# Two token mixers' TensorE work: a hand-written list of steps becomes threads woven into one fixed order, with 16-wide block inverses

## The chip, the cores and the metric

One NeuronCore of one Trainium2 chip runs the whole program in one launch. The metric is the device time of one execution in microseconds (us). Times of a kernel are shown as the median of several executions; one more execution is profiled, and the rows below are from that one.

## The reference

The input is one sequence of 512 frames with 1024 features, all float32. There are two layers. Each layer is a half-weighted SwiGLU feed-forward block (1024 to 2 x 2816 to 1024), a block with two token mixers side by side, and a second feed-forward block. The mixer block, shortened:

```
z = rmsnorm(h) @ w_in[l]                      # columns: r,k,v,w,a,g | q,k,v,o,i,f | two gates of 1024
y_a = rwkv7(...)                              # 8 heads of 64: S = S*w - (S kk) b + v k ; y = S r, frame by frame
y_b = mlstm(...)                              # 4 heads of 128: causal, with input and forget gates, normalised
u = sigmoid(g_a)*(y_a @ br_a) + sigmoid(g_b)*(y_b @ br_b)
h = h + u @ w_out
```

After RWKV7 and mLSTM each head is standardised and gated. The RWKV7 recurrence is evaluated here in chunks of 64 frames, which needs the inverse of a triangular 64x64 matrix for each head and chunk.

## The kernel before

Activations lie transposed: features on the 128 partitions, the 512 frames along the free dimension. A large product is a *projection*: 128 output features from 1024 inputs, eight k-steps into one PSUM bank. For precision each operand is split into a rounded high part and a remainder, so a k-step is three matmuls of 128x512 (L389 to L391). `weights` loads 512 KB of raw weights (two buffers) on SyncE's queue; `cut` makes the high part on ScalarE (L353) and the remainder on VectorE, or on GpSimd while `self.mixing` is set (L354). The split parts of two projections are held at a time. Projections write into three PSUM banks ("mm"), everything else on TensorE into five ("mx").

Between the feed-forward blocks, `mixers` runs. It has 47 projections a layer: one for mixed small columns, two for low-rank inputs, twelve for RWKV (r, k, v for four pairs of heads p), sixteen for mLSTM (q, k, v, o for four heads) and sixteen merge gates. The steps are:

- P (`rwkv_in`) makes decays, keys and receptances of a head pair, with a long chain on VectorE (L800 to L822). X (`rwkv_chunks`) forms the chunk matrices (L845, evacuated at L848 and L849) and transposes (L605). I (`rwkv_inverse`) sends 32x32 blocks through DRAM so that each partition holds whole blocks, inverts them in 31 rounds of two VectorE operations (L884, L886), and sends them back in two layouts, one by way of `td` into t1p. J (`rwkv_merge`) joins 32x32 blocks into 64x64 ones (L902, L906). O (`rwkv_out`) applies the inverse, forms transitions (L938) and runs the recurrence over the chunks (L946, L948, L949, L953). Y (`rwkv_gated`) standardises and gates.
- M, V, S, H make q and k with a short convolution (L659 to L667), the values (ScalarE copy at L672, then transposes), the output gate, and one whole mLSTM head. R computes the mLSTM gates (slab at L645). G is a merge gate's projection, kept in DRAM.

Buffers of the RWKV steps exist twice (`r_set[p % 2]`). A list of steps for each layer, `ORDERS`, sets the order in which they are emitted, with eleven gates among them in layer 0 and five in layer 1; the rest of the gates follow after the last step. The framework's scheduler then orders each engine's queue itself, by emission order, readiness and its own cost model, TensorE's too. At run time every engine takes its queue in order.

## Time and profile before

| | us |
|---|---|
| median of 3 executions | 2565.57 |
| their range | 2559.49 to 4713.14 |
| the profiled execution | 2561.73 |
| its span, first to last instruction | 2560.0 |
| TensorE busy, matmuls | 2455.2 |
| VectorE busy | 1388.7 |
| ScalarE busy | 1050.1 |
| GpSimd busy | 316.0 |

PE is TensorE's matmuls, DVE is VectorE, ACT is ScalarE, POOL is GpSimd; L12 is line 12 of the kernel. Ends of matmuls are modelled by the profiler and overlap the next start, so their spacing is read from the starts. PEclk is the mean granted share of TensorE's clock. A float32 matmul that is not split shows as two records. One of the three executions stands far off the other two and is no measure of the kernel.

### The profile page before, as it was taken

What the parts mean: (1) busy time and instruction counts of PE and PEld (TensorE: products, weight loads), DVE (VectorE), ACT (ScalarE), POOL (GpSimd) and SP (SyncE); (2) the same over time, 40 slices, a digit from 0 to 9 for tenths busy, and PEclk for the clock granted to TensorE, in tenths of its full rate; (3) what the DMA queues carried; (4) which work ended last, traced back from release to release, by engine and by line L of the source; (5) the groups of instructions that cost most, each with busy time, mean ns of one, the idle gap of its engine ahead of it and who ended that gap; (6) DMA issues with size and microseconds to landing.
All of it is one profiled execution on the core that took longest, in us unless ns stands there. A gap on an engine that the chain in (4) does not pass through costs nothing. (4 is left out here: it accounts for less than half of the span.)

```text
span 2560.0 us, 31793 instructions
## 1 busy us (share of the span) xinstructions
PE 2455.2 (96%) x12114; PEld 1983.7 (77%) x12114; DVE 1388.7 (54%) x2421; ACT 1050.1 (41%) x1783; POOL 316.0 (12%) x291
## 2 busy tenths in 40 slices
PE   8999999898989999999999999988999999999997
PEld 7888887676667888888888888767677788888886
DVE  5444445777776644444444434478887555444433
ACT  5333335444546343333343333453555354433322
POOL 0000014322320010000000000143232001000012
PEclk9999999888899999999999999998999999999999
DMA  4222444313332422233332324332213233223232
GB/s 159 93 97 97 116 120 126 103 34 83 105 100 76 147 99 93 97 99 96 94 99 99 99 90 113 117 105 81 80 49 97 77 128 128 95 99 99 92 96 85
DMA packets 127033, 253.46 MB, mean 99 GB/s; under 512 B 55680, under 2 KB 58368, under 8 KB 126880
## 3 DMA queue, kind: packets, MB, share of 16 engines
q1 hardware_dynamic: 126256, 249.79, 31.1%
q8 instruction: 95, 1.56, 0.3%
q10 hardware_dynamic: 624, 1.64, 0.2%
q14 instruction: 58, 0.48, 0.1%
HBM read 230.94 MB, written 20.45 MB: 98 GB/s over the span
## 5 line engine op out<-in xcount | busy, mean ns | idle before, releaser
L353 ACT CAST whi<-wraw 128x512 fp32r<-128x512 f32 (+1 forms) x800 | 485.2, 610 | 1019.8 <-PE mm L390 957.2
L389 PE MATMUL mm<-xh,whi 128*128 128x512 f32 x2160 | 857.2, 397 | 6.0 <-ACT whi L353 5.8
L390 PE MATMUL mm<-xl,whi 128*128 128x512 f32 x2160 | 855.4, 396 | 0.3 <-DVE xl L426 0.2
L391 PE MATMUL mm<-xh,wlo 128*128 128x512 f32 x2160 | 853.4, 395 | 2.2 <-DVE wlo L354 1.3
L354 DVE TENSOR_TENSOR wlo<-wraw,whi 128x512 fp32r<-128x512 f32 (+1 forms) x656 | 458.5, 699 | 542.7 <-ACT whi L353 536.6
L389 PEld LDWEIGHTS mm<-xh,whi 128*128 128x128 f32 x2160 | 411.1, 190 | 95.6 <-ACT whi L353 8.5
L391 PEld LDWEIGHTS mm<-xh,wlo 128*128 128x128 f32 x2160 | 410.6, 190 | 89.3 <-DVE wlo L354 2.2
L390 PEld LDWEIGHTS mm<-xl,whi 128*128 128x128 f32 x2160 | 411.2, 190 | 87.8 <-issue 1.4
L389 PE MATMUL mm<-hh,whi 128*128 128x512 f32 x704 | 273.9, 389 | 0.0
L390 PE MATMUL mm<-hl,whi 128*128 128x512 f32 x704 | 273.9, 389 | 0.0
L391 PE MATMUL mm<-hh,wlo 128*128 128x512 f32 x704 | 273.9, 389 | 0.0
L354 POOL TENSOR_TENSOR wlo<-wraw,whi 128x512 fp32r<-128x512 f32 x144 | 205.4, 1434 | 360.9 <-ACT whi L353 338.6
L438 POOL TENSOR_TENSOR acc<-acc,sq 128x512 f32<-128x512 f32 x36 | 47.9, 1330 | 971.3 <-ACT sq L436 971.3
L390 PEld LDWEIGHTS mm<-hl,whi 128*128 128x128 f32 x704 | 132.2, 188 | 27.7
L391 PEld LDWEIGHTS mm<-hh,wlo 128*128 128x128 f32 x704 | 132.2, 188 | 27.6
L389 PEld LDWEIGHTS mm<-hh,whi 128*128 128x128 f32 x704 | 132.2, 188 | 27.0
L884 DVE TENSOR_TENSOR pr<-ti,mxs 128x16 f32<-128x16 f32 (+30 forms) x248 | 136.9, 552 | 6.5 <-POOL mxs L881 1.2
L469 DVE TENSOR_TENSOR t<-mm,rstd 128x512 f32<-128x512 f32 x88 | 60.8, 691 | 138.7 <-PE mm L391 127.7
L473 DVE TENSOR_TENSOR t<-mm,t 128x512 f32<-128x512 f32 x88 | 60.8, 691 | 132.3 <-PE mm L391 127.7
L886 DVE TENSOR_REDUCE ti<-pr 128x8 f32<-128x16 f32 (+30 forms) x248 | 72.1, 291 | 5.6
L471 ACT ACTIVATE t<-t 128x512 f32<-128x512 f32 x88 | 55.8, 634 | 29.4 <-DVE t L469 29.2
L418 DVE TENSOR_TENSOR hl<-t,hh 128x512 fp32r<-128x512 f32 x88 | 60.9, 692 | 9.9 <-ACT hh L417 2.3
(244 smaller groups left out, 2252.1 us busy)
## 6 DMA issues: line engine op xcount, KB each, us to landing
wraw<-wi SPq DMA_DIRECT2D x94, 512.0 KB, 3.3
wraw<-f2i SPq DMA_DIRECT2D x88, 512.0 KB, 3.2
wraw<-f1i SPq DMA_DIRECT2D x86, 512.0 KB, 3.3
wraw<-f1o SPq DMA_DIRECT2D x32, 512.0 KB, 3.6
wraw<-f2o SPq DMA_DIRECT2D x32, 512.0 KB, 3.5
wraw<-br SPq DMA_DIRECT2D x16, 512.0 KB, 3.3
wraw<-wo SPq DMA_DIRECT2D x16, 512.0 KB, 3.3
wraw<-f1o SPq DMA_DIRECT2D x16, 384.0 KB, 3.2
```

The costliest lines, as they stand in the source:

```text
L353: nc.scalar.copy(out=hi, in_=raw)
L354: eng.tensor_tensor(out=lo, in0=raw, in1=hi.bitcast(F32), op=ALU.subtract)
L389: nc.tensor.matmul(ps, lhsT=hi, rhs=xh, start=first, stop=False)
L390: nc.tensor.matmul(ps, lhsT=hi, rhs=xl, start=False, stop=False)
L391: nc.tensor.matmul(ps, lhsT=lo, rhs=xh, start=False, stop=last)
L418: nc.vector.tensor_tensor(out=lo, in0=x, in1=hi.bitcast(F32), op=ALU.subtract)
L438: eng.tensor_tensor(out=self.acc, in0=self.acc, in1=sq, op=ALU.add)
L469: nc.vector.tensor_tensor(out=g, in0=pg, in1=self.rstd, op=ALU.mult)
L471: nc.scalar.activation(out=s, in_=g, func=AF.Silu)
L473: nc.vector.tensor_tensor(out=p, in0=pu, in1=s, op=ALU.mult)
L884: nc.vector.tensor_tensor(out=pr[:, :, 0 : i + 1], in0=ti[:, 0 : i + 1, :].rearrange("m j c -> m c j"), in1=mx[:, 0 : i + 1, i].unsqueeze( ...
L886: nc.vector.tensor_reduce(out=ti[:, i, :], in_=pr[:, :, 0 : i + 1], axis=mybir.AxisListType.X, op=ALU.add)
```

## The change

The list of steps goes. Each of the four head pairs, the common part, the mLSTM heads, the mLSTM projections, the mLSTM gates and the merge gates becomes a generator, a thread. The new class `Weave` runs them while the program is built. It keeps a planned time for TensorE (`t`) and one for VectorE's queue (`dve`). A thread emits a step, says how long TensorE needs for it (`pe`) or what latency and VectorE time follow (`mark`), and yields what it waits for: a planned time, a flag, a lock on a buffer, or a projection. The first ready thread by rank goes on; while none is ready, one k-step of the current projection is emitted. The merge gates have the last rank and only fill. TensorE's queue is then bound to the order of emission (`manual_schedule`); the other queues stay with the scheduler.

The blocks that are inverted by rounds become 16x16, with 15 rounds; pairs of them are joined to 32x32 by two more sets of small matmuls, and the transposed blocks that came by way of `td` are now made by VectorE's block transpose. The remainder of the weights is always taken on VectorE. The first matmul of each recurrence step (L946) is issued for all chunks ahead into one bank, `sums`, and the step's two others follow it chunk by chunk. The `sums` helper's operands get fixed tiles under a lock.

```diff
-ORDERS = (
-    "G0 P0 G1 S0 G2 X0 G3 G4 P1 G5 G6 X1 I0 G7 V0 R0 J0 O0 Y0 M0 I1 P2 X2 J1 G8 H0 "
...
+class Weave:
...
+    STEP = 0.69
+    def __init__(self, trunk):
+        self.trunk = trunk
+        self.t = self.dve = 0.0
+        self.threads, self.held, self.flags, self.small = [], set(), {}, False
+    def add(self, rank, gen, filler=False):
+        self.threads.append([rank, gen, ("at", 0.0), filler])
+    def mark(self, latency, busy):
+        start = max(self.t, self.dve)
+        self.dve = start + busy
+        return start + latency
+    def pe(self, us):
+        self.t += us + (0.0 if self.small else 0.1)
+        self.small = True
+    def set(self, flag, when=None):
+        self.flags[flag] = self.t if when is None else when
...
+    def ready(self, want):
+        kind, x = want
+        if kind == "at":
+            return x <= self.t
+        if kind == "lock":
+            return x not in self.held
+        if kind == "flag":
+            return x in self.flags and self.flags[x] <= self.t
+        return False
+    def resume(self, th, value=None):
+        try:
+            th[2] = th[1].send(value)
+        except StopIteration:
+            self.threads.remove(th)
+    def run(self):
+        trunk = self.trunk
+        job = None
+        self.threads.sort(key=lambda th: th[0])
+        while job or any(not th[3] for th in self.threads):
+            th = next((th for th in self.threads if self.ready(th[2])), None)
+            if th is not None:
+                if th[2][0] == "lock":
+                    self.held.add(th[2][1])
+                self.resume(th)
+                continue
+            if job is None:
+                th = next((th for th in self.threads if th[2][0] == "proj"), None)
+                if th is not None:
+                    job = [th, trunk.weights(th[2][1]), trunk.mm(), 0]
+                    th[2] = ("job", None)
+                    self.mark(0.0, 1.4)
+            if job is not None:
+                th, w, ps, k = job
+                trunk.product(ps, w, k, trunk.xh[:, k, :], trunk.xl[:, k, :], k == 0, k == KD - 1)
+                self.t += self.STEP + (0.1 if self.small else 0.0)
+                self.small = False
+                job[3] += 1
+                if job[3] == KD:
+                    job = None
+                    self.resume(th, ps)
+                continue
+            times = [th[2][1] for th in self.threads if th[2][0] == "at"]
+            times += [self.flags[th[2][1]] for th in self.threads if th[2][0] == "flag" and th[2][1] in self.flags]
+            self.t = min(times)
...
-        eng = nc.gpsimd if self.mixing else nc.vector
         nc.scalar.copy(out=hi, in_=raw)
-        eng.tensor_tensor(out=lo, in0=raw, in1=hi.bitcast(F32), op=ALU.subtract)
+        nc.vector.tensor_tensor(out=lo, in0=raw, in1=hi.bitcast(F32), op=ALU.subtract)
...
-        steps = {
-            "P": self.rwkv_in, "X": self.rwkv_chunks, "I": self.rwkv_inverse, "J": self.rwkv_merge, "O": self.rwkv_out, "Y": self.rwkv_gated, "M": self.mlstm_in, "V": self.mlstm_values, "S": self.mlstm_output, "H": self.mlstm_head,
-            "G": self.gate_spilled, "R": lambda _: self.mlstm_gates(),
-        }
-        self.mixing = True
-        order = ORDERS[l].split()
-        for s in order:
-            steps[s[0]](int(s[1:]))
...
+        wv = self.wv = Weave(self)
+        wv.add(-1, self.common())
+        for p in range(4):
+            wv.add(p, self.rwkv(p))
+        wv.add(8, self.mlstm_heads())
+        wv.add(9, self.mlstm_projections())
+        wv.add(10, self.mlstm_gates())
+        wv.add(20, self.gates_spilled(early), True)
+        with self.tc.manual_schedule(engines={mybir.EngineType.PE}):
+            wv.run()
...
+    def gates_spilled(self, early):
+        yield "flag", "rows"
+        for i in range(16):
+            ps = yield "proj", self.src[f"g{'ab'[i % 2]}{i // 2}"]
+            g = self.tmp(f"t{1 + i % 2}", 1)
+            self.gate(ps, g)
+            self.nc.sync.dma_start(out=self.gd[i], in_=g)
+            early.add(i)
...
+        yield "at", wv.mark(16.0, 8.0)
         ps = self.mx()
         self.transposes(ps, [slab[:, P * j : P * j + P] for j in range(4)])
...
+    def mlstm_projections(self):
+        nc, l, src, wv = self.nc, self.l, self.src, self.wv
+        yield "flag", "rows"
+        for h in range(4):
+            if h > 0:
+                yield "flag", f"qk{h - 1}"
+            for j, n in enumerate("qk"):
+                i = 4 * j + h
+                ps = yield "proj", src[f"m{n}{h}"]
...
+                qk = wv.mark(7.0, 4.7)
...
+    def rwkv(self, p):
+        wv = self.wv
+        yield "flag", "wa"
+        yield "lock", f"set{p % 2}"
+        yield "lock", "in"
+        yield from self.rwkv_in(p)
+        yield from self.rwkv_chunks(p)
+        wv.free("in")
+        yield "lock", "inverse"
+        yield from self.rwkv_inverse(p)
+        yield from self.rwkv_merge(p)
+        wv.free("inverse")
+        yield "lock", "out"
+        yield from self.rwkv_out(p)
+        wv.free("out")
+        yield "lock", "gated"
+        yield from self.rwkv_gated(p)
+        wv.free("gated")
+        wv.free(f"set{p % 2}")
...
+        self.ready_mx = wv.mark(7.5, 3.4)
+        at = wv.t + 3.0
         for q in range(2):
+            yield "at", at
             Q = slice(4 * q, 4 * q + 4)
             ps = self.mx()
             self.transposes(ps, [bk[:, c, :, :] for c in range(4 * q, 4 * q + 4)])
...
+        nc, wv = self.nc, self.wv
         avr, mn, rbx, s3, dc = self.r_set[p % 2]
-        mx, ti, tz, pr, t1p = self.r_mx, self.r_ti, self.r_tz, self.r_pr, self.r_t1p
-        for g in range(4):
-            nc.sync.dma_start(out=mx[g::4], in_=self.mxd[p])
-        nc.gpsimd.memset(mx.rearrange("m j i -> m (j i)")[:, 0::33], 1.0)
-        nc.gpsimd.tensor_copy(out=ti, in_=self.tid)
-        for i in range(1, 32):
-            nc.vector.tensor_tensor(out=pr[:, :, 0 : i + 1], in0=ti[:, 0 : i + 1, :].rearrange("m j c -> m c j"),
-                                    in1=mx[:, 0 : i + 1, i].unsqueeze(1).broadcast_to([P, 8, i + 1]), op=ALU.mult)
-            nc.vector.tensor_reduce(out=ti[:, i, :], in_=pr[:, :, 0 : i + 1], axis=mybir.AxisListType.X, op=ALU.add)
-        nc.vector.tensor_copy(out=tz, in_=ti.rearrange("m j c -> m c j"))
-        td, zd = self.td[p], self.zd[p]
-        nc.sync.dma_start(out=td, in_=ti[0:64])
+        mx, mt, tz, pr = self.r_mx, self.r_mt, self.r_tz, self.r_pr
+        for g in range(2):
+            nc.sync.dma_start(out=mx[g::2], in_=self.mxd[p])
+        nc.gpsimd.memset(mx.rearrange("m j i -> m (j i)")[:, 0::17], 1.0)
+        nc.scalar.copy(out=mt, in_=mx.rearrange("m j i -> m i j"))
+        nc.gpsimd.tensor_copy(out=tz, in_=self.tid)
+        for i in range(1, 16):
+            nc.vector.tensor_tensor(out=pr[:, :, 0 : i + 1], in0=tz[:, :, 0 : i + 1],
+                                    in1=mt[:, i, 0 : i + 1].unsqueeze(1).broadcast_to([P, 8, i + 1]), op=ALU.mult)
+            nc.vector.tensor_reduce(out=tz[:, :, i], in_=pr[:, :, 0 : i + 1], axis=mybir.AxisListType.X, op=ALU.add)
+        zd = self.zd[p]
         nc.sync.dma_start(out=zd, in_=tz)
-        nc.sync.dma_start(out=t1p[0:32].rearrange("j n (g c) -> j n g c", g=4), in_=td.rearrange("(n g) j c -> j n g c", g=4))
-        for half in range(2):
-            S = slice(32 * half, 32 * half + 32)
-            nc.sync.dma_start(out=mn[S, :, S], in_=zd[64 * half : 64 * half + 64].rearrange("(n g) c j -> (g c) n j", g=4))
+        for q in range(4):
+            S = slice(16 * q, 16 * q + 16)
+            nc.sync.dma_start(out=mn[S, :, S], in_=zd[32 * q : 32 * q + 32].rearrange("(n g) c j -> (g c) n j", g=2))
+        yield "at", self.ready_mx
+        yield "at", wv.mark(14.0, 9.0)
...
+        halves = [slice(32 * h, 32 * h + 32) for h in range(2)]
+        firsts = [slice(32 * h, 32 * h + 16) for h in range(2)]
+        lasts = [slice(32 * h + 16, 32 * h + 32) for h in range(2)]
+        for S in halves:
+            nc.vector.transpose(out=xq[S], in_=mn[S, :, S])
+        yield "at", wv.mark(1.5, 1.2)
+        ps = self.mx()
+        for n in range(16):
+            for S, A in zip(halves, firsts):
+                nc.tensor.matmul(ps[S, 16 * n : 16 * n + 16], lhsT=mn[A, n, S], rhs=xq[A, n, 0:16], start=True, stop=True)
+        wv.pe(1.0)
+        nc.scalar.activation(out=u, in_=ps[0:64, 0:256].rearrange("s (n c) -> s n c", n=16), func=AF.Copy, scale=self.cst[0:64, 3, 64:65])
+        yield "at", wv.t + 1.0
+        ps = self.mx()
+        for n in range(16):
+            for S, A, B in zip(halves, firsts, lasts):
+                nc.tensor.matmul(ps[A, 16 * n : 16 * n + 16], lhsT=u[S, n, :], rhs=mn[S, n, B], start=True, stop=True)
+        for A, B in zip(firsts, lasts):
+            nc.vector.tensor_copy(out=mn[A, :, B], in_=ps[A, 0:256].rearrange("s (n c) -> s n c", n=16))
+        nc.vector.transpose(out=t1p[0:32], in_=mn[0:32, :, 0:32])
+        wv.pe(1.0)
+        yield "at", wv.mark(2.2, 1.7)
...
+        sums = self.mx()
         for c in range(NC - 1):
-            ps = self.mx()
             for R, O, yc, b0 in heads:
-                nc.tensor.matmul(ps[R, 0:CH], lhsT=rbx[:, b0 + c, CH:], rhs=s3[:, b0 + c, yc : yc + CH], start=True, stop=c == 0)
-                if c > 0:
-                    nc.tensor.matmul(ps[R, 0:CH], lhsT=gt[R, c, :], rhs=st[R, c, :], start=False, stop=True)
-            nc.vector.tensor_scalar(out=st[:, c + 1, :], in0=ps[:, 0:CH], scalar1=dc[:, c : c + 1], scalar2=None, op0=ALU.mult)
+                nc.tensor.matmul(sums[R, CH * c : CH * c + CH], lhsT=rbx[:, b0 + c, CH:], rhs=s3[:, b0 + c, yc : yc + CH],
+                                 start=c == 0, stop=c == NC - 2, skip_group_check=True)
+        wv.pe(1.6)
         ps = self.mx()
-        for c in range(1, NC):
-            for R, O, yc, b0 in heads:
-                nc.tensor.matmul(ps[O, CH * c : CH * c + CH], lhsT=st[R, c, :], rhs=r[R, c], start=True, stop=True)
+        for c in range(NC):
+            if c > 0:
+                yield "at", at
+                for R, O, yc, b0 in heads:
+                    if c < NC - 1:
+                        nc.tensor.matmul(sums[R, CH * c : CH * c + CH], lhsT=gt[R, c, :], rhs=st[R, c, :], start=False, stop=True,
+                                         skip_group_check=True)
+                for R, O, yc, b0 in heads:
+                    nc.tensor.matmul(ps[O, CH * c : CH * c + CH], lhsT=st[R, c, :], rhs=r[R, c], start=True, stop=True)
+                wv.pe(0.35)
+            if c < NC - 1:
+                nc.vector.tensor_scalar(out=st[:, c + 1, :], in0=sums[:, CH * c : CH * c + CH], scalar1=dc[:, c : c + 1], scalar2=None, op0=ALU.mult)
+                at = max(at, wv.mark(0.9, 0.3)) if c == 0 else wv.mark(0.9, 0.3)
```

## Rows read from the trace of the kernel before

**Rows 1.** Busy time by stage, whole span: engines, granted clock, DMA share.
```profile
core 0: us, PE busy (x) PEld busy (x) DVE busy (x) ACT busy (x) POOL busy (x), PEclk, DMA share, GB/s
...
368.00:837.00 469.00, 426.03 (x2515) 330.26 (x2514) 325.04 (x659) 234.80 (x422) 127.94 (x117) 0.92 0.31 92
837.00:1642.00 805.00, 805.00 (x3549) 665.89 (x3548) 359.68 (x533) 283.62 (x459) 27.10 (x26) 1.00 0.32 103
1642.00:2098.00 456.00, 415.95 (x2511) 322.07 (x2510) 337.88 (x685) 239.03 (x430) 114.07 (x102) 0.95 0.29 87
```
**Rows 2.** TensorE's waits, 368 to 837 us: total us, times, longest us.
```profile
PE mx L845 <- DVE avr L822: 8.4, 1, 8.4
PE mx L605 <- DVE rbx L849: 7.1, 1, 7.1
PE mx L605 <- ACT t L672: 6.7, 2, 3.9
PE mx L693 <- DVE qk L667: 6.1, 1, 6.1
PE mx L605 <- ACT t L645: 4.9, 1, 4.9
```
**Rows 3.** TensorE's waits, 1642 to 2098 us.
```profile
PE mx L902 <- DMA t1p<-td: 9.3, 3, 3.9
PE mx L605 <- ACT t L645: 6.1, 1, 6.1
PE mx L605 <- DVE rbx L849: 6.1, 4, 3.8
```
**Rows 4.** Busy time in two windows of 16 us, columns as in rows 1.
```profile
512.00:528.00 16.00, 11.12 (x72) 9.02 (x72) 15.38 (x20) 5.13 (x8) 7.19 (x5) 0.88 0.20 67
528.00:544.00 16.00, 16.00 (x126) 13.89 (x126) 8.84 (x28) 5.37 (x10) 0.00 (x0) 0.50 0.01 2
```
**Rows 5.** Timeline of TensorE, 505 to 507 us: start us, us.
```profile
505.44 0.39 PE L390 MATMUL mm<-xl,whi 128*128 128x512 f32 x1
505.85 0.66 PE L605 MATMUL mx<-cst,t 128*128 128x128 f32 x4
506.26 0.47 PE L391 MATMUL mm<-xh,wlo 128*128 128x512 f32 x1
506.58 0.39 PE L389 MATMUL mm<-xh,whi 128*128 128x512 f32 x1
```
**Rows 6.** Timeline of TensorE, 590 to 604 us, a merge at full clock.
```profile
598.03 1.19 PE L902 MATMUL mx<-t1p,mn 32*32 32x32 f32 x32
```
**Rows 7.** Timeline of VectorE, 440 to 500 us.
```profile
447.78 0.15 DVE L884 TENSOR_TENSOR pr<-ti,mxs 128x16 f32<-128x16 f32 x1
447.97 0.17 DVE L886 TENSOR_REDUCE ti<-pr 128x8 f32<-128x16 f32 x1
...
462.03 0.40 DVE L884 TENSOR_TENSOR pr<-ti,mxs 128x128 f32<-128x128 f32 x1
...
463.54 0.27 DVE L886 TENSOR_REDUCE ti<-pr 128x8 f32<-128x128 f32 x1
...
471.59 1.77 DVE L819 SCALAR_TENSOR_TENSOR rw_k<-rw_a,rw_k 128x512 f32<-128x512 f32 x1
...
477.51 1.78 DVE L418 TENSOR_TENSOR sl<-rw_a,sq 128x512 fp32r<-128x512 f32 x1
```
**Rows 8.** Timeline of GpSimd, 470 to 482 us.
```profile
471.08 1.73 POOL L354 TENSOR_TENSOR wlo<-wraw,whi 128x512 fp32r<-128x512 f32 x1
```
**Rows 9.** Timeline of VectorE, 587 to 600 us.
```profile
587.72 0.68 DVE L819 SCALAR_TENSOR_TENSOR rw_k<-rw_a,rw_k 128x512 f32<-128x512 f32 x1
...
599.26 0.68 DVE L903 COPY t1p<-mx 32x512 f32<-32x512 f32 x1 [0.36 <-PE mx L902]
```
**Rows 10.** The page's costliest groups: busy us, mean ns, idle before.
```profile
L884 DVE TENSOR_TENSOR pr<-ti,mxs 128x16 f32<-128x16 f32 (+30 forms) x248 | 136.9, 552 | 6.5 <-POOL mxs L881 1.2
...
L886 DVE TENSOR_REDUCE ti<-pr 128x8 f32<-128x16 f32 (+30 forms) x248 | 72.1, 291 | 5.6
```

296 lines of the change are left out of this document (195 added, 101 removed), and 3 rows, old and new, of the table ORDERS.

## The prediction, made before the change was run

> **What bounds the kernel now.** I cut the span into stages first. From 837 to 1642 us, which is a feed-forward block, the merge of a layer and the next feed-forward blocks, TensorE never idles and its granted clock is 1.00: 3549 matmuls in 805 us, one every 0.227 us [rows 1]. Nothing is to be had there and the change touches nothing there. The two mixers are different. Each stretch in [rows 1] runs from the first mixer projection to the last gate projection of a layer, so both hold the same 47 projections. TensorE is busy 426.0 of 469.0 us in layer 0 and 415.95 of 456.0 in layer 1, so it idles 43.0 + 40.05 = 83 us, and its mean granted clock is 0.92 and 0.95.
>
> What the clock costs comes from the same rows: 0.08 x 469 + 0.05 x 456 = 60 us of full-speed time were not granted. Part of that fell on time in which TensorE idled anyway, so I count four fifths, 48 us. The reader sees both losses side by side in [rows 4]: from 512 to 528 TensorE is busy 11.12 of 16 us, and in the 16 us that follow it is busy throughout, with 126 short matmuls, and is granted 0.50, the lower of its levels (1.2 of 2.4 GHz). It pays twice for a hole: once as idle, once as half speed behind it. So **131 us** (83 + 48) is all that a better order of TensorE's work can give.
>
> Whom TensorE waits for stands in [rows 2] and [rows 3]. No single wait dominates. They are of three kinds. First, short matmuls queued before their input was made, with no product put in between: values copied by ScalarE (L672, 6.7 us), the forget gates' slab (L645, 4.9 in layer 0 and 6.1 in layer 1), the convolution's last operation (L667, 6.1), the first merge matmul behind the DRAM round trip of t1p (9.3 in three waits). Second, VectorE being late with a thing that TensorE had counted on (L822, 8.4; L849, 7.1 and 6.1). Third, little ones. Weight splits are no cause: no wait for L353 or L354 is among these.
>
> **The change part by part.** I sum against the profiled execution, 2561.7 us with a span of 2560.0; the two shown runs that are close to it are 2559.5 and 2565.6 (the latter is the median), so one number serves for all.
>
> *The fixed order.* It takes no product away and adds none. Products are now put into the order one k-step at a time (three matmuls, 0.68 us by [rows 1]) whenever no short step is ready by the plan, and a short step is held back for a stated latency: 1.2 us for the values, 16 us for the gates, 7 us for the convolution, 14 us for inverse and round trip. That is a remedy for the first kind of wait, entry by entry. 47 projections x 24 matmuls x 0.227 = 256 us of products stand in each layer as filler against roughly 140 us of short work and handovers (layer 0: 426 busy, less 30 for the clock, less 256), so the filler lasts. The second kind can come back, since the plan knows VectorE as one queue with rounded costs, and ScalarE and the five mx buffers not at all.
>
> *More handovers.* Where TensorE passes from products to a short group and back, the starts spread: 0.41 us instead of 0.23 going out and 0.32 instead of 0.23 coming back, 0.27 us for the group shown [rows 5]; over others it was nearer to 0.15, so I take 0.2. I counted on TensorE's timeline 77 and 86 such groups in the two layers. From the yields of the new code I count about 26 for each of four head pairs and 20 for the mLSTM and common parts, 125. That is some 90 more groups over both layers: 90 x 0.2 = **18 us added**; 10 to 25 as bounds.
> The Trainium skill has a rule against this part: "TensorEngine Tiling (Array Packing)", section Tiling Modes, says that changing the tiling mode, not just the tile, drains the engine. The rows show some drain, but not a whole one: a product matmul is drawn 0.39 us long and its successor starts 0.32 or 0.41 us later. Were each of the 180 added passages a full drain of 0.39 - 0.23 = 0.16 us, the term would be 29 us and the sum 11 us higher.
>
> *16-wide inverses, on TensorE.* Two new merge steps for each head pair, each 32 matmuls of 16 columns. The nearest row is the old 32-wide merge: 16 float32 matmuls, seen as 32 records, in 1.19 us [rows 6]. 64 records at that rate are 2.4 us a step, 4.8 a pair, 38 us for eight pairs. If the two halves, which sit in different rows and columns of the array, ran fully side by side it would be 19. The order alternates the halves, so I take the middle, **28 us added**. All of it is on the path, since TensorE is what bounds the stage. Nothing that TensorE did before goes away.
>
> *16-wide inverses, on VectorE.* L884 and L886 take 136.9 + 72.1 = 209 us for eight pairs and 31 rounds [rows 10], 26 us a pair. The 15 rounds that stay go from 0.15 + 0.17 us to 0.40 + 0.27 [rows 7], about 15 x 0.5 = 7.4 us a pair. That is 75 us less in each layer. Three block transposes and two copies come in; the nearest row is a 32x512 copy of 0.68 us [rows 9], so some 3 us a pair, 12 a layer. The store and load of td go, and with them the 9.3 us of waits.
>
> *Splits on VectorE.* 144 GpSimd splits become VectorE's at about 0.69 us each (an undisturbed two-input operation of that size takes 0.68 [rows 9]): 54 us in layer 0, where 78 of them lie, and 46 in layer 1. VectorE then has 325 - 75 + 12 + 54 = 316 us and 338 - 75 + 12 + 46 = 321 us of work [rows 1], about what it had, in a stage of some 430 us, 74%. It is not the bound, and TensorE hides it. A gain comes with it that I leave out of the sum: L819 takes 1.77 us at 471.59 while GpSimd's split runs from 471.08 for 1.73 us [rows 7, 8], and 0.68 us at 587.72 [rows 9]. VectorE waits for GpSimd in such places, and they go. It makes VectorE less late, which is the second kind of wait.
> What the move adds is a dependence. A split now stands in VectorE's queue behind the mixers' chains, and the product that reads wlo is next in a fixed order on TensorE; all that stands behind it there, short steps included, waits with it. Between 471.6 and 479.3 us VectorE works without a pause on one pair's chain [rows 7]. The split pieces of two projections are held at once, so a split has one projection, 24 x 0.227 = 5.4 us, and the short work inside it as cover.
>
> *The rest of the mixers.* The sums of states are accumulated ahead in one bank and the steps of the recurrence are spread between products: as many matmuls as before, nothing added. Two small ScalarE operations a pair, with ScalarE busy 235 of 469 us [rows 1], lie beside other work: nothing. DMA issues on SyncE stay at about eleven a pair, nothing. At the start of a layer only three projections can run until the plan has the gates, and some 2 us of idle is likely; it is in the remainder below.
>
> *What stays of the waits.* Of the first kind nothing; of the second (8.4 + 7.1 + 6.1 and the small ones) half, 12 us; for new ones 4 us. That is 16 us of idle, and by the old ratio 48/83 it brings 9 us of lost clock: **25 us**.
>
> Sum: 2560 - 131 + 18 + 28 + 25 = **2500 us**, 2.4% below.
>
> **The rivals.**
> *The waits move (no change).* The plan does not know the mx buffers. The recurrence now holds two of five over its whole length, an mLSTM head holds two over its normalisation, and a chunk step asks for four. The 7.1 us wait for L849 [rows 2] is of this kind, a bank not yet emptied. Against it: the plan holds the transposes back 3 us behind the chunk matmuls, and overlaps of head and recurrence are perhaps two a layer. At 4 x 8 us of such waits and 4 us more at each of eight inverses, 64 us less the 16 in the sum is 48 of idle, and at most 0.58 of that in clock: 2548 to 2576.
> *The clock does not come back (no change).* If single k-steps between bursts of short matmuls do not restore the full level, the 48 us stay while the idle goes: 2500 - 9 + 48 = 2539. Against it: the whole middle stage of [rows 1] ran at 1.00 on products alone, and short work is now mixed with products.
> *Late splits (slower).* The 7.7 us chain of a pair grows with two splits and a convolution beside it to 10 us. If the scheduler puts a split behind all of it, TensorE stands 10 - 5.4 = 4.6 us; for the head pair's chain, the convolutions and the inverse of eight pairs that is 24 x 4.6 = 110 us, less 16 already counted, with clock in the old ratio: 2500 + 94 x 1.58 = 2649. It decides where a run of VectorE work ahead of a split passes 5.4 us, and it makes the kernel over 2% slower from 113/1.58 = 72 us more idle. Against it: in [rows 7] the two halves of one round of the inverse, 462.03 and 463.54, stand 1.5 us apart with other work between them, so queues are mixed by readiness, and a split is ready early.
> *The plan is emptied early (the change does not do what it says).* If padded latencies use up the filler, the end of the last pair stands bare as now. One pair's tail of some 50 us, half idle, in each layer would cost 50: 2550.
>
> **How the numbers follow.** Forecast 0.55 (2475 to 2525), waits moved 0.14, clock 0.08, filler gone 0.07, late splits 0.16. The low end takes the small bounds (19 + 10 us added, 5 left over): 2463, with a little for VectorE freed of GpSimd, **2455**. The high end takes in the three rivals of no change and the milder half of the late splits: **2600**. A measurement of this kernel tells about 2% (51 us) from no change. Below 2510 lies most of the forecast and little else, 0.55; above 2613 most of the late splits and some of the moved waits, 0.14; between them 0.31.
>
> **What would show it.** Right: in both mixer stretches TensorE's idle under 10 us, clock at 0.98 or more, L672, L645, L667 and the t1p load gone from its waits, VectorE near 315 us a layer, L819 at 0.68. The two new merge lines should take 3 to 4 us a pair together. Wrong: waits of product matmuls for VectorE's splits (late splits), of short matmuls for evacuations (moved waits), a clock still at 0.92 without idle, or merges at 5 us and more. The prediction fails upward if the fixed order stalls on many small waits that no row of the old order shows, and downward if short matmuls spread between products cost less than the same in a burst.

## The result: 2454.9 us, 4% below

The changed kernel takes 2454.93 us (median of four, 2451.83 to 2458.45) where the kernel before takes 2562.53 on the same chip: a ratio of 0.959, 95% interval 0.956 to 0.962. (The median of before has the far-off execution of 4713 us in it; the ratio leaves that one out.) The forecast was 2500. The time lies on the low end of the range, 2455, with nothing to spare: two of the four executions are below it. The profiled execution took 2451.83 us, its span is 2450.1.

First the span is cut into stages, as in [rows 1], but from the first mixer projection to the first product with `w_out`, so that the same work lies in the stage of both kernels. Cut like that, the mixer stages of before are 509.1 and 497.9 us long, with the idle of [rows 1], 43.0 and 40.05 us, in them. The two mixer stages before, and then the stages after (columns as in rows 1):

```profile
369.50:878.60 509.10, 466.13 (x2693) 363.31 (x2692) 353.46 (x704) 248.62 (x445) 128.92 (x119) 0.92 0.31 94
...
1642.00:2139.90 497.90, 457.85 (x2695) 356.79 (x2694) 365.66 (x729) 252.64 (x453) 114.07 (x102) 0.96 0.29 88
```
```profile
369.50:815.30 445.80, 431.00 (x3203) 340.47 (x3202) 313.55 (x669) 249.83 (x451) 19.08 (x40) 0.99 0.35 106
815.30:1578.70 763.40, 763.40 (x3365) 631.59 (x3364) 330.70 (x486) 269.18 (x434) 25.50 (x23) 1.00 0.33 102
1578.70:2030.00 451.30, 431.45 (x3207) 340.64 (x3206) 323.24 (x683) 255.43 (x459) 18.92 (x37) 0.99 0.34 104
```

The whole gain lies in the two mixers, 63.3 + 46.6 = 110 us; the stretch between them is busy throughout at a clock of 1.00, as it was. TensorE idles 14.8 and 19.8 us. VectorE, with the splits on it and half of the inverse's rounds gone, is busy 314 and 323 us, where it was 353 and 366. TensorE's waits over the whole span (total us, times, longest):

```profile
PE mm L460 <- ACT whi L424: 10.9, 3, 5.4
PE mx L673 <- ACT t L750: 5.0, 4, 1.5
PE mm L462 <- DVE wlo L425: 5.0, 3, 4.5
PE mx L923 <- ACT wa L872: 3.4, 2, 2.3
...
PE mx L1125 <- ACT s L1036: 2.2, 2, 1.8
...
PE mx L781 <- DVE rbx L1009: 1.7, 1, 1.7
```

Against [rows 2, 3]: L822 (8.4 us), L849 (7.1 and 6.1), L667 (6.1), L645 (4.9 and 6.1) and t1p (9.3) are gone or under 2 us. The values' copy (L672, now L750) still costs 5.0 us, in four short waits. The product's wait for a late remainder `wlo` (L425) is 5.0 us, where the two mixers before had 2.1 in all. Of the first line's 10.9 us, 5.4 lie at the start of the program, outside the mixers.

To compare runs I split each mixer stage's time into three: TensorE's idle; the clock's loss (what its busy stretches at the lower level, 1.2 of 2.4 GHz, took over their length at full clock, by the spacing of the same instruction's starts); and the rest, TensorE's *work* at full clock, handovers included. The split is of the profiled execution, which can stand some us off the median of its kernel (b_all's is 9 us above, a_step's and b_dve's 7 below). Sums of both layers in us:

| run | ratio to before | stages | idle | clock | work |
|---|---|---|---|---|---|
| before | 1 | 1006.9 | 83.1 | 46.3 | 877.5 |
| after | 0.959 | 897.2 | 34.6 | 7.1 | 855.5 |
| after, repeated | 0.960 | 897.1 | 33.4 | 8.7 | 855.0 |
| a_free | 0.956 | 890.1 | 27.2 | 7.2 | 855.8 |
| a_hp | 0.961 | 903.8 | 37.3 | 11.6 | 855.0 |
| a_gate | 0.965 | 914.1 | 42.0 | 21.1 | 851.2 |
| a_pool | 0.971 | 927.9 | 54.0 | 19.0 | 855.0 |
| a_mix | 0.972 | 936.9 | 45.6 | 28.2 | 863.1 |
| a_step | 0.982 | 951.1 | 38.4 | 20.1 | 892.7 |
| b_all | 0.965 | 919.9 | 31.1 | 23.0 | 865.9 |
| b_16dve_pairs | 0.975 | 939.1 | 35.3 | 16.9 | 886.9 |
| b_rec | 0.988 | 972.4 | 88.7 | 34.5 | 849.2 |
| b_dve | 0.989 | 973.4 | 66.6 | 25.3 | 881.5 |
| b_16 | 1.000 | 1005.2 | 68.0 | 39.1 | 898.0 |

So the change gave 48.5 us of idle, 39 of clock and 22 of work, 110 in all. The sum had 67 of idle, 39 of clock, and 46 of work the other way. The experiments named a_ are edits of the changed kernel, those named b_ of the kernel before.

### The profile page after: what moved, and what is told of

Read it like the earlier page. It is cut to its first block, busy times and chain, and to the rows that moved or that the text cites. A ratio compares the mean times of both kernels' runs of the same rounds, so it can differ in the third digit from the quotient of the medians.

```text
span 2450.1 us, 33539 instructions
## 1 busy us (share of the span) xinstructions
PE 2394.5 (98%) x13138; PEld 1945.7 (79%) x13138; DVE 1306.7 (53%) x2341; ACT 1054.2 (43%) x1795; POOL 111.1 (5%) x147
## 4 chain that ended last, share of the span: by engine, by line
PE 62%; DVE 3%; ACT 2%; DMA 1%; issue 0%; DVEq 0%; POOL 0%; ACTq 0%; SPq 0%; POOLq 0%
PE mm L460 20%; PE mm L462 19%; PE mm L461 19%; DMA yd<-avr 0%; PE mx L673 0%; DMA t<-yd 0%; PE mx L1156 0%; DVE wlo L425 0%; PE mx L781 0%; PE mx L796 0%; DMA t<-mats 0%; PE mx L1144 0%; ACT L512 0%; ACT L513 0%; PE mx L1102 0%
## 5 line engine op out<-in xcount | busy, mean ns | idle before, releaser
L460 PE MATMUL mm<-xh,whi 128*128 128x512 f32 x2160 | 862.7, 399 | 11.0 <-ACT whi L424 10.9
L425 DVE TENSOR_TENSOR wlo<-wraw,whi 128x512 fp32r<-128x512 f32 (+1 forms) x800 | 555.8, 697 | 580.9 <-ACT whi L424 573.1
L461 PE MATMUL mm<-xl,whi 128*128 128x512 f32 x2160 | 844.7, 391 | 0.0
L460 PEld LDWEIGHTS mm<-hh,whi 128*128 128x128 f32 x704 | 132.2, 188 | 27.2
L508 POOL TENSOR_TENSOR acc<-acc,t 128x512 f32<-128x512 f32 x36 | 47.9, 1330 | 1194.3 <-ACT t L506 1180.1
L488 DVE TENSOR_TENSOR hl<-t,hh 128x512 fp32r<-128x512 f32 x88 | 61.0, 693 | 9.6 <-ACT hh L487 2.0
L487 ACT CAST hh<-t 128x512 fp32r<-128x512 f32 x88 | 54.7, 622 | 24.6 <-DVE t L543 24.6
L495 ACT ACTIVATE xh<-h,vec 128x512 fp32r<-128x512 f32 x48 | 34.6, 723 | 44.9 <-DVE h L555 33.7
L460 PE MATMUL mm<-yh,whi 128*128 128x512 f32 x128 | 50.5, 400 | 2.5 <-DVE gb L640 1.6
```

Of the source, the lines that this page charges most:

```text
L425: nc.vector.tensor_tensor(out=lo, in0=raw, in1=hi.bitcast(F32), op=ALU.subtract)
L460: nc.tensor.matmul(ps, lhsT=hi, rhs=xh, start=first, stop=False)
L461: nc.tensor.matmul(ps, lhsT=hi, rhs=xl, start=False, stop=False)
L487: nc.scalar.copy(out=hi, in_=x)
L488: nc.vector.tensor_tensor(out=lo, in0=x, in1=hi.bitcast(F32), op=ALU.subtract)
L495: nc.scalar.activation(out=self.xh[:, i, :], in_=h, func=AF.Copy, scale=gain)
```

## Experiments

### Is it the fixed order? (a_free, a_hp, a_gate)

a_free leaves the threads and their order of emission, but lets the framework's scheduler order TensorE's queue:

```diff
-        with self.tc.manual_schedule(engines={mybir.EngineType.PE}):
-            wv.run()
+        wv.run()
```

> The changed kernel with the one line left out that binds TensorE's queue to the order of emission; threads, 16-wide inverses and splits on VectorE stay, and the scheduler orders TensorE's queue again. Theory (the bound order fills the holes): the scheduler pulls products ahead of short steps, idle in the two mixer stages goes from 28 us back to 50 or more and the clock below 0.98, 2490 to 2540 us. Rival (VectorE has become punctual, so any order is good): within 15 us of the changed kernel's 2455.

Measured: 2446.03 us, ratio 0.956 (0.952 to 0.960). The theory that the binding fills the holes fell; the time is where the rival put it. But the run says less about the order itself than its name: counted on the two timelines, the scheduler took nearly the same order on its own. Of the 3768 records of short matmuls in both mixers, 3373 have exactly as many products ahead of them as in after. Its waits in the trace:

```profile
PE mx L672 <- ACT t L713: 8.5, 2, 4.6
PE mm L460 <- ACT whi L424: 8.5, 3, 5.4
```

The gates' slab (L645 of rows 2 and 3, here L713) is waited for again, 8.5 us, which the fixed order does avoid. Products wait only 0.4 us in all for a remainder, and the total idle is 7 us smaller. This is the fastest kernel that ran; its interval overlaps that of after (0.956 to 0.962), so that binding the order costs time is not shown, only that it brings none once the threads have emitted it.

a_hp gives both split operations a higher priority in the scheduler:

```diff
-        nc.scalar.copy(out=hi, in_=raw)
-        nc.vector.tensor_tensor(out=lo, in0=raw, in1=hi.bitcast(F32), op=ALU.subtract)
+        with self.tc.high_priority(offset=400):
+            nc.scalar.copy(out=hi, in_=raw)
+            nc.vector.tensor_tensor(out=lo, in0=raw, in1=hi.bitcast(F32), op=ALU.subtract)
```

> The changed kernel with the weight splits, both halves on ScalarE and VectorE, moved 400 places forward in the scheduler's priority. Late splits: TensorE's holes of 4.5 and 4.7 us at the start of the two mixers (a split behind the gates' chain) go, with the half clock behind them, 2440 to 2450 us. Rival: the chains now stand behind splits that nobody waits for yet, and short steps come late, 2465 to 2490.

Measured: 2459.22 us, ratio 0.961 (0.956 to 0.966), no gain; the time lies between the two expectations. Its idle is 37.3 us; the product's wait for `wlo` is no more among the longest, and others come in (the merge's ScalarE operand 5.9 us, a sum of squares 5.6).

a_gate starts the mLSTM gates' chain only with the fourth projection, since at the start of a mixer that chain stands ahead of a split:

```diff
-        yield "flag", "misc"
+        yield "flag", "fourth"
...
+                    self.jobs += 1
+                    if self.jobs == 4:
+                        self.set("fourth")
```

> The changed kernel with the mLSTM gates' thread started only when the fourth projection's weights have been issued, so that no split of it stands behind the gates' chain. Late splits at the start: the holes of 4.5 and 4.7 us and the half clock behind them (6.8 us each) go, 6 to 14 us faster than the changed kernel. Rival (the hole only moves, to the first mLSTM projection that waits for the gates' rows): within 4 us.

Measured: 2469.08 us, ratio 0.965 (0.962 to 0.968), 12 us slower than the repeat of after on that chip; both expectations missed. The holes moved:

```profile
PE mx L1005 <- DVE avr L967: 6.8, 2, 3.7
PE mx L484 <- ACT sq L490: 6.0, 1, 6.0
PE mm L463 <- ACT whi L427: 5.3, 1, 5.3
```

Idle rose by 9 and the clock's loss by 12 us against that repeat. The 35 us of idle that are left are not the fault of one chain; what would take them away stays open.

### The splits (a_pool, b_dve)

a_pool puts the mixers' splits back on GpSimd:

```diff
...
+        eng = nc.gpsimd if self.mixing else nc.vector
...
-        nc.vector.tensor_tensor(out=lo, in0=raw, in1=hi.bitcast(F32), op=ALU.subtract)
+        eng.tensor_tensor(out=lo, in0=raw, in1=hi.bitcast(F32), op=ALU.subtract)
...
```

> The changed kernel with the mixers' weight splits on GpSimd again, nothing else. Theory of the order: VectorE's operations are stretched where GpSimd reads (L961 above 0.68 us again), TensorE's idle grows by 10 to 25 us, 2465 to 2490 us. Rival (the punctual VectorE is the cause of the gain): 2500 us and more. Third (the split in VectorE's queue costs as much as the port): 2445 to 2460.

Measured: 2484.65 us, ratio 0.971 (0.967 to 0.975): by the two ratios 29 us given back, 19 in idle and 12 in clock, none in work. TensorE's instructions stand in the same order as in after, one for one in both mixers, so this difference owes nothing to the order. It is in the range of the first theory and short of the rival's 2500: under the threads the place of the splits is worth 29 us, not the whole gain. L819 of [rows 7, 9] (L965 here, L961 in after) shows why. Its eight instructions, minimum/median/maximum ns, in a_pool and in after:

```profile
L965 DVE SCALAR_TENSOR_TENSOR rw_k<-rw_a,rw_k x8: 676/1226/1781, 414.2 to 1921.8; 128x512 f32<-128x512 f32 x8
```
```profile
L961 DVE SCALAR_TENSOR_TENSOR rw_k<-rw_a,rw_k x8: 671/681/684, 417.6 to 1893.1; 128x512 f32<-128x512 f32 x8
```

Beside GpSimd's splits the same operation takes up to 1.78 us, without them 0.67 to 0.68 each time. The Trainium skill, "SBUF — State Buffer", section SBUF: two separate sides, says that a VectorE operation with two SBUF inputs and a GpSimd operation that reads SBUF lock a port pair against each other; the two lines agree.

b_dve makes the same move alone, in the kernel before:

```diff
-        eng = nc.gpsimd if self.mixing else nc.vector
+        eng = nc.vector
```

> The kernel before with the mixers' weight splits on VectorE alone. Theory of the order: with 31 rounds of the inverse in the same queue splits come late, VectorE's load in a mixer goes from 325 to some 335 us net of what GpSimd no longer stretches, and the time is 2555 to 2600 us. Rival (the port is the cause): 2530 us or less, with L819 at 0.68 us.

Measured: 2533.51 us, ratio 0.989 (0.986 to 0.992), 29 us gained with no thread and no new list. The first theory fell; the rival's 2530 was missed by 3.5 us, with L819 at 0.68 us as it said. VectorE took over 53 and 45 us of splits and is hardly busier than the 353.46 and 365.66 us of before, because its other operations are no longer stretched (by summed durations in layer 0 the inverse's rounds fall from 105 to 88 us and the rest from 254 to 229):

```profile
368.40:847.70 479.30, 451.41 (x2692) 353.68 (x2691) 354.71 (x781) 249.65 (x445) 19.10 (x41) 0.97 0.33 99
1611.10:2105.20 494.10, 455.38 (x2695) 354.54 (x2694) 361.37 (x795) 252.00 (x453) 18.92 (x36) 0.96 0.29 89
```

Here the late splits of the third rival do appear:

```profile
PE mm L391 <- DVE wlo L354: 17.3, 8, 6.0
```

and the timeline shows the longest of them, a split behind rounds of the inverse and a convolution:

```profile
1966.78 0.70 DVE L667 SCALAR_TENSOR_TENSOR qk<-ee,qk 128x512 f32<-128x512 f32 x1
1967.38 0.41 DVE L886 TENSOR_REDUCE ti<-pr 128x8 f32<-128x240 f32 x1
1967.69 0.70 DVE L354 TENSOR_TENSOR wlo<-wraw,whi 128x512 fp32r<-128x512 f32 x1
...
1968.44 0.79 PE L391 MATMUL mm<-xh,wlo 128*128 128x512 f32 x1 [5.99 <-DVE wlo L354]
```

### The 16-wide inverse (b_16)

The inverse and merges of the change in the kernel before, without threads and without the splits' move:

```diff
-        for i in range(1, 32):
+        for i in range(1, 16):
...
+        for n in range(16):
+            for S, A in zip(halves, firsts):
+                nc.tensor.matmul(ps[S, 16 * n : 16 * n + 16], lhsT=mn[A, n, S], rhs=xq[A, n, 0:16], start=True, stop=True)
...
+        nc.vector.transpose(out=t1p[0:32], in_=mn[0:32, :, 0:32])
```

> The kernel before with the 16-wide inverses alone, two more merges and two block transposes included. Theory of the order: VectorE has 60 us less in each mixer and the t1p waits go, but holes at short steps stay, and the merges add 16 us to TensorE: 2535 to 2560 us. Rival (VectorE's lateness was the cause of the holes): under 2520.

Measured: 2560.47 us, ratio 1.000 (0.998 to 1.002), at the top of the first theory's range and far from the rival's 2520. Alone it is worth nothing: 22 us less idle and clock loss, 20 more work.

### All parts without threads (b_all, with after repeated)

b_all is the kernel before with its `ORDERS`, its scheduler and its steps, plus three parts of the change: the 16-wide inverse, the splits on VectorE, and the recurrence's new form (b_rec, below).

> The kernel before with all three of the other parts (new recurrence, 16-wide inverses, splits on VectorE) but with the old list of steps: no threads, no bound order. If the parts add up as they did singly (-32, 0, -29 us) it is at 2500 us. Theory (16-wide inverses matter once the splits are on VectorE, because splits no longer come late behind 31 rounds): 2480 to 2495 us, idle 45 to 60 us, and the threads are worth 25 to 45 us. Rival (threads are worth nothing without a bound order and nothing with it): 2460 us or less.

> The changed kernel once more, on the same chip as the others of this call, to set the one without a bound order and the one with later gates beside it: 2445 to 2460 us.

Measured on the same chip: b_all 2466.0 us, ratio 0.965 (0.961 to 0.968); after again 2456.81, ratio 0.960 (0.957 to 0.963). Nine tenths of the gain need neither the threads nor a fixed order; for the threads (with the fixed tiles of `sums`, which b_all lacks too) about 9 us remain, at the edge of what these intervals tell apart. Neither expectation was met: 2466 lies below the theory and above the rival. By the table the idle is the same with and without threads (31.1 and 33.4 us); what the threads have less of is clock loss (8.7 against 23.0) and work (855.0 against 865.9), in a profiled execution of b_all that stands 9 us above its median. That the parts bring more together than singly comes from layer 1 alone: its stage is 33 us shorter in b_all, where the three single parts come to 3 us longer in sum; in layer 0 it is 54 us shorter, where they come to 73.

### The recurrence (b_rec, a_step, a_mix)

b_rec makes only the new form of the recurrence in the kernel before: the 128-row matmuls of all chunks first, in one bank, and then per chunk the 64-row ones of both heads:

```diff
+        sums = self.mx()
         for c in range(NC - 1):
-            ps = self.mx()
             for R, O, yc, b0 in heads:
-                nc.tensor.matmul(ps[R, 0:CH], lhsT=rbx[:, b0 + c, CH:], rhs=s3[:, b0 + c, yc : yc + CH], start=True, stop=c == 0)
-                if c > 0:
-                    nc.tensor.matmul(ps[R, 0:CH], lhsT=gt[R, c, :], rhs=st[R, c, :], start=False, stop=True)
+                nc.tensor.matmul(sums[R, CH * c : CH * c + CH], lhsT=rbx[:, b0 + c, CH:], rhs=s3[:, b0 + c, yc : yc + CH],
+                                 start=c == 0, stop=c == NC - 2, skip_group_check=True)
...
```

> The kernel before with the new recurrence alone: the first matmul of each chunk issued for all chunks ahead into one bank, the other two following chunk by chunk; list of steps, 32-wide inverses and GpSimd splits stay. Theory (grouping by array shape shortens TensorE's work by some 15 us a layer): 2530 to 2545 us. Rival (the old spacing was a wait for VectorE, which stays as it is without weaving): within 8 us of 2562.

Measured: 2530.02 us, ratio 0.988 (0.985 to 0.991), 32 us gained by the ratio, at the near end of the theory's range, and 28 of them are TensorE's work. No number of matmuls changed.

a_step is the reverse: the old form inside the threads, with a product's k-step between chunks:

```diff
-        sums = self.mx()
...
+            ps = self.mx()
+            for R, O, yc, b0 in heads:
+                nc.tensor.matmul(ps[R, 0:CH], lhsT=rbx[:, b0 + c, CH:], rhs=s3[:, b0 + c, yc : yc + CH], start=True, stop=c == 0)
+                if c > 0:
+                    nc.tensor.matmul(ps[R, 0:CH], lhsT=gt[R, c, :], rhs=st[R, c, :], start=False, stop=True)
...
```

> The changed kernel with the recurrence in its old form under the threads: each chunk's four matmuls together in a bank of their own, both array shapes in turn, and the states applied at the end. Theory (grouping matmuls of one shape is what made TensorE's own work shorter, 107 ns a record to 34 for the one line and 87 to 7 for the other): the two lines are back at 85 ns or more each and the kernel is 20 to 35 us slower, 2475 to 2490. Rival (the old spacing was the wait for VectorE's state, which woven products now cover): spacing under 50 ns and within 8 us of 2455.

Measured: 2513.67 us, ratio 0.982 (0.978 to 0.987). By the ratios it gives back 58 us, more than the 20 to 35 expected; in the profiled executions 37 lie in work, 13 in clock, 4 in idle. TensorE's timeline for one chunk step, in a_step and then in after:

```profile
539.12 0.33 PE L1168 MATMUL mx<-s,rbx 128*64 128x64 f32 x2
539.38 0.33 PE L1170 MATMUL mx<-st,gt 64*64 64x64 f32 x2
539.63 0.33 PE L1168 MATMUL mx<-s,rbx 128*64 128x64 f32 x2
539.89 0.33 PE L1170 MATMUL mx<-st,gt 64*64 64x64 f32 x2
540.15 0.50 PE L460 MATMUL mm<-xh,whi 128*128 128x512 f32 x1
```
```profile
529.28 1.03 PE L1166 MATMUL mx<-s,rbx 128*64 128x64 f32 x28
530.24 2.50 PE L796 MATMUL mx<-v,pt 128*128 128x129 f32 x20
...
538.15 0.27 PE L1175 MATMUL mx<-st,gt 64*64 64x64 f32 x2
538.16 0.27 PE L1178 MATMUL mx<-avr,st 64*64 64x64 f32 x2
538.25 0.23 PE L1175 MATMUL mx<-st,gt 64*64 64x64 f32 x2
538.27 0.22 PE L1178 MATMUL mx<-avr,st 64*64 64x64 f32 x2
538.42 1.19 PE L1086 MATMUL mx<-xq,mn 16*32 16x16 f32 x64
```

Read the starts. In a_step each matmul (two records) holds TensorE 0.26 us, four of them 1.03. In after the 14 first matmuls of seven chunks take 0.96 us together, and a chunk's four others 0.27.

a_mix keeps the one bank and the 64-row pairing, and puts only the 128-row matmuls of a chunk back next to its others:

```diff
-        for c in range(NC - 1):
-            for R, O, yc, b0 in heads:
-                nc.tensor.matmul(sums[R, CH * c : CH * c + CH], lhsT=rbx[:, b0 + c, CH:], rhs=s3[:, b0 + c, yc : yc + CH],
...
+            if c < NC - 1:
+                for R, O, yc, b0 in heads:
+                    nc.tensor.matmul(sums[R, CH * c : CH * c + CH], lhsT=rbx[:, b0 + c, CH:], rhs=s3[:, b0 + c, yc : yc + CH],
...
```

> The changed kernel in which only the place of the recurrence's first matmul is moved: each chunk's 128-row matmul stands again right before the chunk's 64-row ones, but in the one shared bank, and the states are applied chunk by chunk as in the change. Theory (taking turns between array shapes is the cost): both lines at 80 ns a record or more, 2475 to 2500 us. Rival (a bank of its own for each chunk, with its evacuation, was the cost): spacing below 45 ns, within 8 us of the changed kernel.

Measured: 2485.06 us, ratio 0.972 (0.969 to 0.975), 28 us slower than the repeat of after on that chip. The profiled executions stand 39 us apart: 8 in work (the 128-row line goes from 34 to 67 ns a record, the 64-row lines stay), 12 in idle and 20 in clock. The time is in the theory's range, but its 80 ns for both lines was too much: one turn a chunk more is put back, not the three of the old form.

### Bank or turn, and the pair of VectorE parts (b_16dve_pairs)

The kernel before with the 16-wide inverse and the splits on VectorE. Layer 0 keeps the old recurrence; in layer 1 each chunk keeps a bank of its own, but both heads' 128-row matmuls go first and then both 64-row ones:

```diff
...
+                for R, O, yc, b0 in heads:
+                    nc.tensor.matmul(ps[R, 0:CH], lhsT=rbx[:, b0 + c, CH:], rhs=s3[:, b0 + c, yc : yc + CH], start=True, stop=c == 0)
                 if c > 0:
+                    for R, O, yc, b0 in heads:
+                        nc.tensor.matmul(ps[R, 0:CH], lhsT=gt[R, c, :], rhs=st[R, c, :], start=False, stop=True)
```

> The kernel before with 16-wide inverses and splits on VectorE together, without threads and without the new recurrence. In layer 0 the recurrence is as before; in layer 1 each chunk keeps its own bank, but both heads' 128-row matmuls come first and then both 64-row ones, one turn of array shape a chunk instead of two. Singly the two parts gave 0 and -29 us, the new recurrence -33, all three -92. Theory (the two help each other: short inverses let splits on VectorE pass): layer 0's stage at 468 us or less (509.0 before, 479.3 with the splits alone, 495.4 with the inverses alone) and about 2500 us in all. Rival (they add up only with the recurrence's gaps gone): 479 us or more and 2520 to 2535. For the recurrence in layer 1: theory (turns of array shape): its two lines take about 65 ns a record together counted with layer 0's 106 and 87. Rival (adding onto an output that was just written, in a bank of its own): 85 ns or more as in layer 0.

Measured: 2494.44 us, ratio 0.975 (0.972 to 0.978). Layer 0's stage is 468.4 us against 509.1 before, and stage and time are what the theory of VectorE said. The recurrence's two lines take 39 ns a record in layer 1 and 97 in layer 0, 68 together, which also fits the turns. TensorE's timeline in layer 0 and in layer 1:

```profile
537.33 0.33 PE L967 MATMUL mx<-st,gt 64*64 64x64 f32 x2
537.59 0.33 PE L965 MATMUL mx<-s,rbx 128*64 128x64 f32 x2
537.84 0.27 PE L967 MATMUL mx<-st,gt 64*64 64x64 f32 x1
...
1737.42 0.33 PE L973 MATMUL mx<-st,gt 64*64 64x64 f32 x4
1737.68 0.34 PE L970 MATMUL mx<-s,rbx 128*64 128x64 f32 x4
1737.95 0.50 PE L391 MATMUL mm<-xh,wlo 128*128 128x512 f32 x1
```

A run of one shape takes 0.26 us in both, though it is one matmul in layer 0 and two in layer 1. So the price hangs on the number of runs, that is on the turns between 128-row and 64-row shapes, not on matmuls and not on the bank. Part of it is that two heads' matmuls of one shape, put next to each other, run side by side: their records start 7 ns apart. The turn at 1737.68 is between matmuls of which the second does not read or add to what the first wrote, so a wait for an output just written doesn't explain it; no run tells only these two apart.

The second result is layer 0, where only the two VectorE parts differ from before: idle and clock loss fall from 43.0 + 29.2 = 72 us to 11.9 + 9.2 = 21, where after has 14.8 + 3.6 = 18. Singly the parts take 32 (b_dve) and 22 (b_16) from that layer's 72, so there they add up. TensorE's two longest waits in layer 0 are now

```profile
PE mm L391 <- DVE wlo L354: 5.5, 3, 2.9
PE mx L605 <- ACT pt L720: 1.5, 2, 1.3
```

and of the five in [rows 2], 33.2 us, those for L822, L672 and L645 are gone and those for L849 and L667 are at 0.4 us or less. In layer 1 (57 us before) the parts take 6 and 0 singly, and 26 together with the regrouped recurrence. What makes layer 1 indifferent to one part alone stays open.

One rival stays as well. In the b_ runs the list of steps is as before, but TensorE's queue is not: the scheduler orders it anew. Counted on the timelines, 945 of 1114 records of the short matmuls that both kernels have in layer 0 have moved past more than three product matmuls against before, some past 25, a whole projection. How much of the 51 us is the punctual VectorE itself and how much the order that the scheduler then found, these runs do not separate. For the splits alone a_pool does, where the order is identical; for the inverse no run does.

## Why the prediction was right, and where its steps were not

**What bounds the kernel**: right. The middle stage did not move, and all came from the two mixers' idle, clock and short work.

**131 us at stake, 25 left over**: 42 are left over, 34.6 of idle and 7.1 of clock. The clock's part (39 us won) came out exactly, but by luck: at the old ratio 48/83, by which it was reckoned, 34.6 us of idle would have brought 20 us of clock loss, not 7. Idle is 18 us larger than forecast. What is left of [rows 2, 3] is small: the values' copy 5.0 us, where nothing was put, and L849 1.7, where 12 were put for VectorE's lateness. Nearly all else are waits that [rows 2, 3] do not have, for which 4 were put. Two holes, 9.2 us, stand at the start of the mixers, where only few projections can run and the gates' chain (L711, L488) and others fill VectorE:

```profile
393.20 1.22 DVE L711 TENSOR_TENSOR_SCAN t<-t 4x512 f32<-4x512 f32 x1
...
393.64 0.40 PE L461 MATMUL mm<-xl,whi 128*128 128x512 f32 x1
...
396.41 0.72 DVE L488 TENSOR_TENSOR rc<-t,rc 4x512 fp32r<-4x512 f32 x1
397.15 0.75 DVE L574 SCALAR_TENSOR_TENSOR sg<-zt,onemu,sg 128x512 f32<-128x512 f32 x1
397.81 0.69 DVE L425 TENSOR_TENSOR wlo<-wraw,whi 128x512 fp32r<-128x512 f32 x1
...
398.56 0.80 PE L462 MATMUL mm<-xh,wlo 128*128 128x512 f32 x1 [4.52 <-DVE wlo L425]
```

TensorE stands 4.5 us, and the matmul behind the hole is drawn at twice the length, as in [rows 4]; layer 1 begins with 4.7 us of the same kind, for `whi` from ScalarE. I had put 2 us there.

**Who won the idle**: this is the step that failed. The prediction gave the 131 us, but for the 9.3 of t1p, to "a better order of TensorE's work" and left VectorE freed of GpSimd out of the sum. The runs give it the other way round: all three parts without threads bring nine tenths of the time (b_all), the splits alone are worth 29 us with TensorE's order held (a_pool), and in layer 0 the splits and the shorter inverse bring 51 of the 54 us of idle and clock under the old list of steps (b_16dve_pairs). Unbinding TensorE's order costs nothing (a_free), though there the order hardly changed. The second kind of wait, VectorE late, thus weighed far more than the prediction gave it, also in waits that ended at ScalarE (L672 and L645 are gone from layer 0). That it was the main cause is shown for layer 0 but for the scheduler's new order, and not for layer 1.

**The rest of the mixers, "as many matmuls as before, nothing added"**: the count is right, the cost is not. Spacing at full clock gives the recurrence's three lines 52.6 us before and 22.8 after: 30 us less work that the sum did not have. By the rows, 28 records of one shape take 0.96 us and four take 0.26, so a record without a turn is (0.96 - 0.26)/24 = 0.029 us and a turn costs 0.26 - 4 x 0.029 = 0.14 us, and 0.20 from two records, in which a lone head has nothing beside it; three turns less in six steps of eight pairs are 144 x 0.14 to 0.20 = 20 to 29 us. The prediction did weigh the rule of the Trainium skill ("TensorEngine Tiling (Array Packing)", section Tiling Modes: a change of mode drains the engine), but at the handovers from products, where it speaks against the change. Inside the recurrence, which the diff regroups, it speaks for it. The trace agrees with the rule there, with 0.14 to 0.20 us a turn.

**More handovers, +18 us**: 2 or 3. Counted as in the prediction there are 163 groups between products before and 175 after; I had expected 253 from the yields, but a thread whose next time has come goes on without a product in between. That the rows show "some drain, but not a whole one" does not fit the way out in [rows 5], where the successor starts 0.41 us behind a matmul drawn 0.39 us long.

**The merges, +28 us**: 16. The start of L1086's 64 records to the next product is 1.12 us in

```profile
538.42 1.19 PE L1086 MATMUL mx<-xq,mn 16*32 16x16 f32 x64
539.54 0.50 PE L460 MATMUL mm<-xh,whi 128*128 128x512 f32 x1
...
541.13 0.97 PE L1094 MATMUL mx<-mn,u 32*16 32x16 f32 x64
542.03 0.50 PE L460 MATMUL mm<-xh,whi 128*128 128x512 f32 x1
```

and 0.90 us for L1094: 17 and 14 ns a record, half of the 35 ns of [rows 6], with the two halves side by side. The low bound of 19 was the right end. These three steps, 30 + 16 + 12 us, make 58 of the 68 us by which TensorE's work was mis-sized; transposes that follow one another more often (20 us in place of 26) make most of the rest.

**VectorE**: 316 and 321 us forecast, 314 and 323 measured, but the two do not measure the same stretch. The forecast starts from [rows 1], up to the last gate projection; the measured stage goes on to `w_out`, and there before has 353.46 and 365.66 us. With the same terms the forecast for it is 345 and 349, some 31 and 25 us too high. The agreement is chance; what is missing is the stretching by GpSimd that b_dve shows to go. The splits and what is left of the inverse in layer 0 (busy us, mean ns; then VectorE's idle ahead):

```profile
L425 DVE TENSOR_TENSOR wlo<-wraw,whi 128x512 fp32r<-128x512 f32 x110 | 74.7, 685 | 24.1 <-ACT whi L424 20.7 <-PE mx L673 2.5 <-PE mx L796 0.9
...
L1062 DVE TENSOR_TENSOR pr<-tz,mt 128x16 f32<-128x16 f32 (+14 forms) x60 | 13.9, 232 | 5.9 <-ACT mt L1059 4.4
L1064 DVE TENSOR_REDUCE tz<-pr 128x8 f32<-128x16 f32 (+14 forms) x60 | 13.6, 227 | 1.5
```

**The rivals.** *Late splits* exist, but VectorE more often waits for the split's input (20.7 us ahead of L425 in layer 0) than TensorE for the split (5.0 us, where 110 was the price). The rival named the right place for a kernel that moves the splits and keeps 31 rounds: 17.3 us in b_dve. *Waits move* and *filler gone* did not come: no wait for an evacuated bank is over 2 us. *The clock* came back, 0.99 in both stages. Of the prediction's own signs, idle under 10 us a stretch, the values' copy gone and 3 to 4 us of merges a pair (2.0 came) failed.

**The time itself.** That it still lies on the edge of the range is luck too. The low end of 2463, and 2455 with a little off, had 29 us of work added and 5 us left over. Measured were 22 us of work gained, 51 us better, and 42 left over, 37 us worse: two errors that for the most part cancel. The prediction saw a way down, short matmuls that cost less, but in their spreading between products; it was their regrouping by shape.

## What to carry to other kernels

Before an order is blamed for an engine's idle time, look at whether the engine that feeds it is stretched by a neighbour: here the removal of GpSimd's splits and of half the inverse's rounds from a list of steps left as it was gave, in layer 0, most of what a new scheduler seemed to give. An experiment that frees an order is read only after looking at what order came of it: a_free hardly changed it, the b_ runs did. Parts of a change must be tried together as well as singly: by their ratios the three were worth 62 us one by one and 91 together. Small matmuls are counted in runs of one shape, not in matmuls: group them by shape across heads and chunks before spreading them.

## What the runs showed of the chip that was not expected

A turn between 128-row and 64-row float32 matmuls of 64 columns costs TensorE 0.14 to 0.20 us, as much as five to seven records without a turn (29 ns each). The 64-row matmuls of L1175 and L1178, of two heads and in one run, start 10 to 20 ns apart in two groups 0.1 us apart, four of them in 0.27 us, and a pair of 16-column matmuls in different halves comes down to 14 to 17 ns a record. VectorE took over 98 us of splits from GpSimd in b_dve and was no busier for it: 716 us in the two mixer stages, 719 before. In a_mix and a_gate, edits of 8 us of work or less cost 28 and 12 us, most of it in idle and in clock behind the new holes: where a stage mixes short work with products, a small hole is paid twice, as in [rows 4], also in the changed kernel.
